# A hybrid attention block: the first attention stage in written order on four engines, the merge's gate weights loaded earlier, and a new order at the merge's head

## The chip, the cores and the metric

The kernel runs on one core of one Trainium2 chip. The metric is the device time of one execution in microseconds (us). The core's engines are PE (matmuls), DVE (vector), ACT (scalar and activation), POOL (a second, slower vector engine) and SP, which here only issues DMAs. Each engine works through its own queue in order; between queues there are semaphores.

## The reference

One layer of a decoder block over 528 positions (16 learned meta tokens ahead of 512 tokens, width 1024). One projection of the normed input feeds two attention branches of 16 heads, MLA and FoX (a forgetting attention whose logits get a cumulative gate). Each branch's output is multiplied by silu of its z, projected, gated by a sigmoid and summed:

```python
u = rmsnorm(h, pre_norm_g[l])
proj = u @ w_in[l]
(cq, ckv, k_pe_raw, z_mla, fq, fk, fv, f_logit, z_fox, gate_a, gate_b) = jnp.split(proj, split_idx, axis=-1)
...
y_mla = (o_mla * jax.nn.silu(z_mla)) @ w_br_mla[l]
...
y_fox = (o_fox * jax.nn.silu(z_fox)) @ w_br_fox[l]
mixed = (jax.nn.sigmoid(gate_a) * y_mla + jax.nn.sigmoid(gate_b) * y_fox) @ w_out[l]
h = h + rmsnorm(mixed, post_norm_g[l])
```

## The kernel before

**Numbers in two parts.** Weights and activations are split into a high and a low part, and each product is three matmul passes (high by high, high by low, low by high). A weight tile of 128 x 1024 is loaded by SP (`wload`, L133, tile `wraw`), its high part is cast by ACT (`wsplit`, L142, `wh`), and its low part is a subtraction on POOL or DVE (`split_lo`, L118, `wl`). All three tiles come from the pool `wp`, three buffers each, so that a load waits until an older tile is free.

**The stages.** After a front phase (norm, transposes, small projections) come 16 attention stages, two heads each, FoX and MLA by turns. A stage is: the scores of query blocks 0 to 2 (`scores(0)`, called s0), then of block 3 (s1): PE writes `st`, DVE takes it out with a running minimum (L665, `sf`, `nb`), ACT takes the exponentials (L673, which also sums them into `su`). Then the norm (`norm(0)`, `norm(1)`, called n0 and n1): DVE scales `su` and takes its reciprocal `ri` (L681, L682), ACT writes the high part of the weights `pn` (L700), DVE the low part (L701), POOL both parts of the meta columns (L687 to L692), and SP issues a DMA transpose `pt<-pn` for each block and head, eight in a stage (L706). The values (`values`, PE's `ov`) follow in the next stage between s0 and s1, since they need `pt`. Between these pieces PE runs the fills: steps of projections for coming stages, each step one block of matmuls. In the first stages they are z (the gates of silu: ACT and DVE make `sil` from it, L617 and L618), `mq` and `mk` (MLA queries and keys, cut into high and low, `hlq` and `hlk`, by ACT L255 and DVE L118), v, and vt (the values transposed, cut into `vp` and `vm`) and so on. A step's first matmul makes the unit's weights, and also calls the loads of the next three units.

**The rope.** `pe_unit` computes the rotated part of the queries for eight heads at a time. `rest` turns the two halves x on POOL (L544, `gT<-gT`), casts the high part on ACT (L545), splits off the low part on POOL (L118) and writes four pieces to `qpe_dram` (L548). For each pair of MLA heads `q_done` then loads `QP` from there (L507), which the scores of the next MLA stage read.

**Who sets the order.** In the attention stages PE runs in written order (`manual_schedule`), and a scheduler with priorities sets the order of the others. From the merge on, all engines run in an order written as strings of short words (`go`): w, b and u are the operands of the merge's products and of its y units (L load, S scale, q square sums, s a sum of two parts, h and l the high and low operand), G makes the next gate's weights and asks for the load of the one after, g is one step of a gate's matmuls (three of them), y a step of a y unit, M the mix of gate and y, O one of the eight units of W_out prepared ahead of the end. The gates are `pg` on PE and a tanh on ACT (L437, L449, `th`). `Weights.scale` uses `sum` (PE, ones by the partial square sums `yss`) and makes `ysc` from it on DVE (L112 and on).

Of the kernel before, what the change touches and what calls it, by code (L numbers as in the profile page):

```python
# [54 lines left out]
def block_kernel(ctx: ExitStack, tc: tile.TileContext, x, meta_tokens, pre_norm_g, w_in, fox_forget_b,  # L55
# [81 lines left out]

    def wsplit(ld, keep=None, eng=None):

        u, raw, parts, n = ld  # L140
        wh, wl = ((keep or wp).tile([128, 1024], F32R, tag=t, name=f"{t}{u}") for t in ("wh", "wl"))
        nc.scalar.copy(wh[:, :n], raw[:, :n])  # L142
        split_lo(eng or nc.gpsimd, wl[:, :n], raw[:, :n], wh[:, :n])
        return [(wh[:, o : o + w], wl[:, o : o + w]) for o, w in parts]
# [4 lines left out]
    def weights(srcs, wrap):  # L149

        st = {}

        def load():
            if "l" not in st:
                st["l"] = wload(srcs())

        def get(eng=None):
            load()
            return wrap(wsplit(st["l"], eng=eng))
        get.load = load  # L160
        return get
# [26 lines left out]
    def unit(name, getw, act, nk, sls, done):  # L188

        st = {}  # L190
        out = []
        for i, sl in enumerate(sls):
            n = sl.stop - sl.start
            for k in range(nk):
                def fn(i=i, sl=sl, k=k, n=n):
                    if "w" not in st:
                        st["w"] = getw()
                        for load in getattr(out[0][1], "nxt", ()):
                            load()
# [8 lines left out]
                out.append((3 * n / 2.4, fn))  # L208
        if hasattr(getw, "load"):
            out[0][1].load = getw.load  # L210
        return out
# [244 lines left out]


    with ExitStack() as att:

# [32 lines left out]
        wuqh = wuq.rearrange("p k (h e) -> p k h e", e=NOPE + ROPE)  # L492

        def q_mla(pr):
            kv = wukv.rearrange("p (h a e) -> p a h e", a=2, e=HD)

            def wrap(w):
                mw[pr] = w
                return (lambda k: w[k][0]), (lambda k: w[k][1])
            get = weights(lambda: [wuqh[:, k, 2 * pr : 2 * pr + 2, 0:NOPE] for k in range(2)]  # L500
                          + [kv[:, i, 2 * pr : 2 * pr + 2, :] for i in range(2)], wrap)

            halves = hl_done(("q", 0, pr), S, S)

            def q_done(i, ps):
                halves(i, ps)
                nc.sync.dma_start(f32(QP), qpe_dram[2 * pr : 2 * pr + 2].rearrange("h i x f s -> (h i x f) s"))  # L507
            return unit(f"mq{pr}", get, cq_act, 2, REAL, q_done)
# [3 lines left out]
        def pe_unit(g):  # L512
# [27 lines left out]

            def rest():

                for x in range(2):
                    nc.gpsimd.tensor_tensor(out=tt[:, x], in0=tt[:, x], in1=tt[:, 3 - x], op=(ALU.subtract, ALU.add)[x])  # L544
                    nc.scalar.copy(rr[:, x], tt[:, x])  # L545
                    split_lo(nc.gpsimd, rr[:, 2 + x], tt[:, x], rr[:, x])
                    for i in range(2):
                        nc.sync.dma_start(qpe_dram[8 * g : 8 * g + 8, i, x], f32(rr[:, 2 * i + x]))  # L548
            return out, [(0, rest)]

# [71 lines left out]
        def attention(br, pr):  # L622
# [20 lines left out]
            def scores(g):  # L643
# [4 lines left out]
                def fn():  # L648
# [4 lines left out]
                    for ib, parts in enumerate(banks):  # L653
# [5 lines left out]
                        for b, c0, w, o in parts:  # L659
                            m0 = 384 - 128 * b + c0  # L660
                            for h in range(2):
                                nb = sums["nb"][:, h, b : b + 1]

                                with tc.high_priority(offset=100):
                                    nc.vector.tensor_tensor_reduce(  # L665
                                        out=sf_of(h, b)[:, c0 : c0 + w], in0=ps[h][:, o : o + w],
                                        in1=maskt[:, m0 : m0 + w], scale=-scale, scalar=3.0e38 if c0 == 0 else nb,
                                        op0=ALU.add, op1=ALU.min, accum_out=nb)
                    with tc.high_priority(offset=60):
                        for b in GRP[g]:  # L670
                            for h in range(2):
                                sf = sf_of(h, b)
                                nc.scalar.activation(sf, sf, AF.Exp, bias=sums["nb"][:, h, b : b + 1], scale=-1.0,  # L673
                                                     accum_out=sums["su"][:, h, b : b + 1])
                return fn

            def norm(g):
                def fn():
                    b0, nb_ = GRP[g][0], len(GRP[g])
# [13 lines left out]
                    for b in GRP[g]:  # L693
                        for h in range(2):
# [3 lines left out]
                                      for i in range(2))  # L698
# [46 lines left out]
        v, vts[1, 0] = v_unit(1, 0)  # L745
        pe, pe_rest = pe_unit(0)
        first = v + gate_unit() + pe
        fills = []
        for si, (br, pr) in enumerate(stages):
# [16 lines left out]
            if si == 0:  # L766
                fill[2:2] = pe_rest
            if si == 1:
                pe, pe_rest = pe_unit(1)
                fill[9:9] = pe + pe_rest  # L770
            fills.append(fill)
# [6 lines left out]
        for si, (br, pr) in enumerate(stages):  # L778
            s0, s1, n0, n1, va = attention(br, pr)

            for fn in [s0] + late + [s1]:
                fn()

            fill = fills[si]
            run(fill[:4])
            n0()
# [14 lines left out]

    def wout_unit(n, c, keep=None):
        return by_k(wunit([wout[:, 2 * c : 2 * c + 2, 512 * n : 512 * n + 512]], keep)[0], 2)

    E_ = mybir.EngineType
    with ExitStack() as mg:
# [191 lines left out]
        def go(plan):  # L998

            for t in plan.split():  # L1000
# [28 lines left out]
                elif k == "O":  # L1029
                    pre.append(wout_unit(0, len(pre)))  # L1030
                else:
# [139 lines left out]
```

## Time and profile before

| | us |
|---|---|
| runs of the kernel before | 629.81, 633.15, 635.74 |
| median | 633.15 |
| profiled execution, its own time | 629.45 |
| its span in the trace | 627.6 |
| mean granted TensorE clock of its core | 0.996 |
| busy: PE, DVE, ACT, POOL | 601.6, 381.7, 383.4, 193.6 |

The span runs from the first to the last instruction of the trace; all times of rows are from its start. A row of the timeline has the start, the time, the engine, the line, the operation, the tiles (out<-in), the shape and the count; where the engine stood idle before it, the idle time and what ended it follow in brackets. A row with a count over 1 has the time of the whole block. The front phase ends near 56 us, the first attention stage starts near 72, the merge's head lies near 425 to 455, the y units from about 520 to 590, the last projection and norm behind them.

### The profile page before, as it was taken

The numbers are of one execution on the slowest core, as the hardware profiler recorded it, in microseconds if no ns is written. First come the engines' busy times: TensorE is split into PE (matmuls) and PEld (weight loads), VectorE is DVE, ScalarE is ACT, GpSimd is POOL, SyncE is SP. The second block draws the span as 40 slices with busy tenths as digits, with TensorE's granted clock in tenths as the row PEclk, the third lists the DMA queues.
The fourth block names the chain that finished last, engine by engine and source line by source line (L and its number), as shares of the span: only waits on it lengthen the run. The fifth ranks groups of instructions, "written<-read, shape, count | busy, mean of one in ns | idle before, by whom it ended". The sixth has DMA issues, their size and how long they took to land.

```text
span 627.6 us, 11566 instructions
## 1 busy us (share of the span) xinstructions
PE 601.6 (96%) x4058; PEld 493.9 (79%) x4058; DVE 381.7 (61%) x1013; ACT 383.4 (61%) x838; POOL 193.6 (31%) x239
## 2 busy tenths in 40 slices
PE   2999989999999999999999999999899999999996
PEld 2879767988988889889889888887688876655885
DVE  3757557377367565664774774664977774448234
ACT  5656478378477676774884785774867754245421
POOL 3334643734344353252443353410000000004700
PEclk9999989999999999999999999999999999999999
DMA  8443557866656688477467566657153128314302
GB/s 268 141 84 86 112 141 190 191 151 159 154 126 154 152 146 153 124 165 183 84 157 166 137 152 150 145 125 231 38 149 96 55 71 261 110 40 156 107 33 101
DMA packets 204865, 85.40 MB, mean 136 GB/s; under 512 B 122684, under 2 KB 197820, under 8 KB 204808
## 3 DMA queue, kind: packets, MB, share of 16 engines
q1 hardware_dynamic: 204808, 84.67, 54.2%
q8 instruction: 32, 0.52, 0.4%
q14 instruction: 25, 0.20, 0.1%
HBM read 55.21 MB, written 4.26 MB: 95 GB/s over the span
## 4 chain that ended last, share of the span: by engine, by line
PE 87%; ACT 4%; DMA 3%; DVE 2%; SPq 1%; POOL 1%; issue 1%; DVEq 0%; POOLq 0%; ACTq 0%
PE z L92 12%; PE pg L92 12%; PE v L92 8%; PE st L92 8%; PE fk L92 8%; PE po L92 7%; PE fq L92 7%; PE py L92 6%; PE ov L92 5%; PE yx L92 3%; PE psm L92 3%; PE yy L92 2%; PE mq L92 2%; PE mk L92 1%; DMA wsr<-in_w_in_dram 1%; PE vt L95 1%
## 5 line engine op out<-in xcount | busy, mean ns | idle before, releaser
L118 POOL TENSOR_TENSOR wl<-wraw,wh 128x1024 fp32r<-128x1024 f32 (+1 forms) x62 | 137.8, 2226 | 300.7 <-ACT wh L142 290.5
L142 ACT CAST wh<-wraw 128x1024 fp32r<-128x1024 f32 (+1 forms) x74 | 72.8, 987 | 82.1 <-issue 35.6
L673 ACT ACTIVATE sf<-sf,nb 128x144 f32<-128x144 f32 (+3 forms) x128 | 71.9, 565 | 3.0 <-DVE nb L665 3.0
L700 ACT ACTIVATE pn<-sf,ri 128x128 f16<-128x128 f32 (+3 forms) x128 | 61.9, 552 | 15.0 <-ACT sf L673 14.8
L701 DVE SCALAR_TENSOR_TENSOR pn<-sf,ri,pn 128x128 f16<-128x128 f32 (+3 forms) x128 | 66.0, 555 | 7.9 <-ACT pn L700 7.9
L92 PE MATMUL pg<-uTh,wh 128*128 128x512 f32 x128 | 52.1, 407 | 1.6 <-DVE ysc L112 1.6
L92 PE MATMUL z<-uTh,wh 128*128 128x512 f32 x128 | 51.4, 402 | 0.0
L92 PE MATMUL pg<-uTh,wl 128*128 128x512 f32 x128 | 50.1, 391 | 0.5 <-DVE wl L118 0.5
L92 PE MATMUL z<-uTl,wh 128*128 128x512 f32 x128 | 50.6, 395 | 0.0
L92 PE MATMUL z<-uTh,wl 128*128 128x512 f32 x128 | 50.4, 394 | 0.0
L92 PE MATMUL pg<-uTl,wh 128*128 128x512 f32 x128 | 49.9, 390 | 0.0
L665 DVE CUSTOM_DVE_ANT_0 sf<-st,maskt 128x272 f32<-128x272 f32 (+2 forms) x128 | 48.5, 435 | 0.0
L92 PE MATMUL st<-hlk,hlq 64*128 64x272 f32 (+3 forms) x480 | 47.9, 307 | 0.4 <-DVE nb L665 0.2
L92 PE MATMUL py<-g,yw 128*128 128x512 f16 x192 | 42.6, 379 | 0.6 <-DVE yw L934 0.6
L92 PEld LDWEIGHTS st<-hlk,hlq 64*128 64x128 f32 x480 | 35.3, 185 | 6.7 <-ACT wh L142 2.5
L92 PE MATMUL fk<-uTl,wh 128*128 128x256 f32 (+1 forms) x128 | 36.6, 286 | 0.0
L92 PE MATMUL fk<-uTh,wh 128*128 128x256 f32 (+1 forms) x128 | 36.5, 285 | 0.0
L92 PE MATMUL v<-uTh,wh 128*128 128x256 f32 (+1 forms) x128 | 36.5, 285 | 0.0
L92 PE MATMUL fk<-uTh,wl 128*128 128x256 f32 (+1 forms) x128 | 36.5, 285 | 0.0
L92 PE MATMUL v<-uTl,wh 128*128 128x256 f32 (+1 forms) x128 | 36.4, 285 | 0.0
L92 PE MATMUL v<-uTh,wl 128*128 128x256 f32 (+1 forms) x128 | 36.4, 284 | 0.0
L687 POOL TENSOR_TENSOR mt<-sf,ri 128x96 f32<-128x96 f32 (+1 forms) x32 | 9.5, 298 | 86.3 <-DVE ri L682 46.5
(291 smaller groups left out, 1512.0 us busy)
## 6 DMA issues: line engine op xcount, KB each, us to landing
wraw<-in_w_in_dram SPq DMA_DIRECT2D x56, 512.0 KB, 4.4
yraw<-in_w_br_fox_dram SPq DMA_DIRECT2D x8, 512.0 KB
yraw<-in_w_br_mla_dram SPq DMA_DIRECT2D x8, 512.0 KB, 4.5
wraw<-in_w_out_dram SPq DMA_DIRECT2D x8, 512.0 KB, 3.5
qpe_dram<-gT SPq DMA_DIRECT2D x8, 256.0 KB
QP<-qpe_dram SPq DMA_DIRECT2D x8, 256.0 KB, 2.8
pt<-pn SPq DMA_TRANSPOSE x128, 2.7
xr<-in_x_dram SPq DMA_DIRECT2D x4, 512.0 KB
```

What stands on the lines that cost most here:

```text
L92: nc.tensor.matmul(*a, **k)
L95: nc.tensor.transpose(*a)
L118: eng.tensor_tensor(out=lo, in0=src, in1=f32(hi), op=ALU.subtract)
L142: nc.scalar.copy(wh[:, :n], raw[:, :n])
L665: nc.vector.tensor_tensor_reduce(out=sf_of(h, b)[:, c0 : c0 + w], in0=ps[h][:, o : o + w], in1=maskt[:, m0 : m0 + w], scale=-scale, scalar ...
L673: nc.scalar.activation(sf, sf, AF.Exp, bias=sums["nb"][:, h, b : b + 1], scale=-1.0, accum_out=sums["su"][:, h, b : b + 1])
L687: nc.gpsimd.tensor_tensor(out=mt, in0=src, in1=ri.unsqueeze(3).broadcast_to([128, 2, nb_, META]), op=ALU.mult)
L700: nc.scalar.activation(hi, sf, AF.Copy, scale=rib)
L701: nc.vector.scalar_tensor_tensor(out=lo, in0=sf, scalar=rib, in1=hi, op0=ALU.mult, op1=ALU.subtract)
```

## The change

It has four parts, and the matmuls stay the same in number and shape.

1. **Stage one in written order.** For si == 0 the engines PE, POOL, ACT and DVE run in the order of the code, from the making of the weights of the first z unit to the first four fill steps. `scores` returns the exponentials as a function of their own. `pe_unit` returns `turn` (both turns of the rope on POOL, x = 1 first) and `rest(x)` (cast, low part, DMAs), which are called between the exponentials of blocks 0, 1 and 2. The weights of zb are made ahead, with the low part on DVE behind the norm of blocks 0 to 2 (`lo[0]()`). The first QP load is issued within the norm, behind the transposes of block 0.
2. **Gate weights.** Ahead of the last values, `mgates[1]` and `mgates[2]` are asked for, where it was `mgates[1]` alone.
3. **The head of the merge.** A new plan string.
4. **The y units.** The gate steps stand behind y0, y2, y4 and y5 (before: y0 to y3), G stands in y0, y2 and y4 (before: y0, y1, y2), and the O in the y units is in y5 instead of y6 with its low part on DVE instead of POOL.

```diff
-    def wsplit(ld, keep=None, eng=None):
+    def wsplit(ld, keep=None, eng=None, later=None):
...
-        split_lo(eng or nc.gpsimd, wl[:, :n], raw[:, :n], wh[:, :n])
+
+        def lo():
+            split_lo(eng or nc.gpsimd, wl[:, :n], raw[:, :n], wh[:, :n])
+        if later is None:
+            lo()
+        else:
+            later.append(lo)
...
+        def make(*a):
+            if "w" not in st:
+                st["w"] = getw(*a)
+                for load in getattr(out[0][1], "nxt", ()):
+                    load()
...
             def q_done(i, ps):
                 halves(i, ps)
-                nc.sync.dma_start(f32(QP), qpe_dram[2 * pr : 2 * pr + 2].rearrange("h i x f s -> (h i x f) s"))
+                if pr:
+                    load_qp(pr)
...
-            def rest():
-
-                for x in range(2):
+            def turn():
+
+                for x in (1, 0):
                     nc.gpsimd.tensor_tensor(out=tt[:, x], in0=tt[:, x], in1=tt[:, 3 - x], op=(ALU.subtract, ALU.add)[x])
-                    nc.scalar.copy(rr[:, x], tt[:, x])
-                    split_lo(nc.gpsimd, rr[:, 2 + x], tt[:, x], rr[:, x])
-                    for i in range(2):
-                        nc.sync.dma_start(qpe_dram[8 * g : 8 * g + 8, i, x], f32(rr[:, 2 * i + x]))
-            return out, [(0, rest)]
+
+            def rest(x):
+                nc.scalar.copy(rr[:, x], tt[:, x])
+                split_lo(nc.gpsimd, rr[:, 2 + x], tt[:, x], rr[:, x])
+                for i in range(2):
+                    nc.sync.dma_start(qpe_dram[8 * g : 8 * g + 8, i, x], f32(rr[:, 2 * i + x]))
+            return out, turn, rest
...
                     for b in GRP[g]:
+                        if b == 1:
+                            mid()
                         for h in range(2):
...
+            with ExitStack() as head:
+                if si == 0:
+                    head.enter_context(tc.manual_schedule(engines={E_.PE, E_.Pool, E_.Activation, E_.DVE}))
+                    za, q, zb = early
+                    turn, rest = rope0
+                    za.make()
+                    q.make()
+                    lo = []
+                    turn()
+                    s0()
+                    zb.make(nc.vector, lo)
+                    e0({(0, 1): lambda: rest(1), (1, 1): lambda: rest(0)})
+                    s1()
+                    n0(lambda: load_qp(0))
+                    lo[0]()
+                    e1()
+                    run(fill[:4])
...
-        mgates[1].load()
+        for g in mgates[1:3]:
+            g.load()
...
-        go("w0L w1L G b1s7 b1hA b1hB g g b1lA w0q0 g b1lB b1s6 w0q1 g g G b1s4 g g b1s5 b1hC w0S g w0s7 w0hA g w0hB b1lC g w0lA "
-           "g w0lB b1hD g w0s6 g G w0s5 w0s3 g w0hC g b1lD g w0hD g w0lC g w1q0 g w0lD g g w1q1 g g G g g g g g g g g g")
+        go("w0L b1s7 G b1hA b1hB g g b1lA w0q0 g g b1lB b1s6 g g b1s4 w0q1 G w1L g g g w0S b1hC w0s7 b1s5 g w0hA g w0hB b1lC "
+           "g w0lA g b1hD g w0lB w0s6 g G w0s5 w0s3 g w0hC b1lD g w0hD g w0lC g w1q0 g w0lD g g w1q1 g g G g g g g g g g g")
...
-            plan = (f"y{i}0 {n}L y{i}1 {j + 'S' if i else ''} y{i}2 {j}h {mix[0]} y{i}3 {j}l y{i}4 {mix[1]} y{i}5 {n}q y{i}6 {'G' if i < 3 else ''} y{i}7 "
-                    + "g " * (8 * (i < 4)) + ("O" if i == 6 else ""))
+            plan = (f"y{i}0 {n}L y{i}1 {j + 'S' if i else ''} y{i}2 {j}h {mix[0]} y{i}3 {j}l y{i}4 {mix[1]} y{i}5 {n}q y{i}6 "
+                    f"{'G' if i in (0, 2, 4) else 'O' if i == 5 else ''} y{i}7 " + "g " * (8 * (i in (0, 2, 4, 5))))
```

Three places where the rows of an engine move. (The lines of the changed file differ from those before by 11 to 45; L706 is L729 now, L548 is L566, L665 is L683, L673 is L693, L681 and L682 are L702 and L703, L701 is L722, L618 is L636, L822 is L867 and L846 is L891.)

SP, in the first attention stage, before. `wraw_1016` are weights of the second pair's keys, `CT` the cumulative gates of the FoX branch; the two transposes with 128x3x128 are block 0's, those with 5 block 1's, with 7 block 2's, with 9 block 3's:

```order
L548 DMA qpe_dram<-gT_684 8x16x512
L133 DMA wraw_1016<-in_w_in_dram 128x8x128
L548 DMA qpe_dram<-gT_684 8x16x512 x3
L269 DMA CT<-c_dram 2x528 x2
L507 DMA QP<-qpe_dram 128x512
L706 DMA_TRANSPOSE pt_661<-pn_659 128x3x128
L706 DMA_TRANSPOSE pt_662<-pn_659 128x3x128
L706 DMA_TRANSPOSE pt_661<-pn_659 128x5x128
L706 DMA_TRANSPOSE pt_662<-pn_659 128x5x128
L706 DMA_TRANSPOSE pt_661<-pn_659 128x7x128
L706 DMA_TRANSPOSE pt_662<-pn_659 128x7x128
```

The same place in the changed kernel, where `wraw_887` stands for `wraw_1016`:

```order
L566 DMA qpe_dram<-gT_684 8x16x512 x4
L280 DMA CT<-c_dram 2x528
L729 DMA_TRANSPOSE pt_661<-pn_659 128x3x128
L729 DMA_TRANSPOSE pt_662<-pn_659 128x3x128
L280 DMA CT<-c_dram 2x528
L507 DMA QP<-qpe_dram 128x512
L729 DMA_TRANSPOSE pt_661<-pn_659 128x5x128
L729 DMA_TRANSPOSE pt_662<-pn_659 128x5x128
L729 DMA_TRANSPOSE pt_661<-pn_659 128x7x128
L133 DMA wraw_887<-in_w_in_dram 128x8x128
L729 DMA_TRANSPOSE pt_662<-pn_659 128x7x128
L133 DMA wraw_1194<-in_w_in_dram 128x8x128
```

The four writes of the rope now stand together, block 0's transposes stand ahead of the QP load, and the load of `wraw_887` has moved from between the rope's writes to between block 2's two transposes; another load follows it.

DVE, from the first reciprocals of stage one to the first split of queries and keys, before:

```order
L681 TENSOR_SCALAR su_827<-su_827 128x2x3
L682 RECIPROCAL ri_828<-su_827 128x2x3
L681 TENSOR_SCALAR su_827<-su_827 128x2
L682 RECIPROCAL ri_828<-su_827 128x2
L701 SCALAR_TENSOR_TENSOR pn_659<-sf_829,ri_828,pn_659 128x128 x2
L701 SCALAR_TENSOR_TENSOR pn_659<-sf_829,ri_828,pn_659 128x2x128 x2
L701 SCALAR_TENSOR_TENSOR pn_659<-sf_829,ri_828,pn_659 128x3x128 x2
L701 SCALAR_TENSOR_TENSOR pn_660<-sf_870,ri_828,pn_660 128x4x128 x2
L618 SCALAR_TENSOR_TENSOR sil_963<-sil_963,z_903 128x512
L598 TENSOR_TENSOR vp_664<-vt_966,vp_664 128x8x64
L608 TENSOR_TENSOR vm_666<-vm_973,vm_666 16x128
L118 TENSOR_TENSOR hlq_1008<-mq_988,hlq_1008 128x512
```

The same place in the changed kernel:

```order
L703 RECIPROCAL ri_848<-su_847 128x2x3
L722 SCALAR_TENSOR_TENSOR pn_659<-sf_849,ri_848,pn_659 128x128 x2
L722 SCALAR_TENSOR_TENSOR pn_659<-sf_849,ri_848,pn_659 128x2x128 x2
L722 SCALAR_TENSOR_TENSOR pn_659<-sf_849,ri_848,pn_659 128x3x128 x2
L118 TENSOR_TENSOR wl_885<-wraw_806,wh_884 128x1024
L702 TENSOR_SCALAR su_847<-su_847 128x2
L703 RECIPROCAL ri_848<-su_847 128x2
L636 SCALAR_TENSOR_TENSOR sil_983<-sil_983,z_957 128x512
L616 TENSOR_TENSOR vp_664<-vt_986,vp_664 128x8x64
L118 TENSOR_TENSOR hlq_1005<-mq_998,hlq_1005 128x512
L626 TENSOR_TENSOR vm_666<-vm_993,vm_666 16x128
L722 SCALAR_TENSOR_TENSOR pn_660<-sf_903,ri_848,pn_660 128x4x128 x2
```

The low part of zb's weights (`wl_885`) has come in from POOL and stands behind the pn of blocks 0 to 2; the pn of block 3 (`pn_660`) has moved behind `sil`, `vp`, `hlq` and `vm`.

DVE at the head of the merge, before; `bop1` are the operands of the FoX branch, `gT` its gated values, `wl` the low part of a gate's weights:

```order
L846 SCALAR_TENSOR_TENSOR bop1A<-gT_688,gsc,bop1A 128x2048
L846 SCALAR_TENSOR_TENSOR bop1B<-gT_688,gsc,bop1B 128x1024
L822 TENSOR_TENSOR gT_688<-gT_688 128x4x256
L118 TENSOR_TENSOR wl_5630<-wraw_5601,wh_5629 128x1024
L822 TENSOR_TENSOR gT_688<-gT_688 128x4x256 x2
L112 TENSOR_SCALAR ysc_5590<-sum_5645 128x1
L114 TENSOR_SCALAR ysc_5590<-ysc_5590 128x1
L115 RECIPROCAL ysc_5590<-ysc_5590 128x1
L869 TENSOR_SCALAR ysc_5590<-ysc_5590,gsc 128x1
L822 TENSOR_TENSOR yraw_5587<-yraw_5587 128x512
L846 SCALAR_TENSOR_TENSOR bop1C<-gT_688,gsc,bop1C 128x2048
```

The same place in the changed kernel:

```order
L891 SCALAR_TENSOR_TENSOR bop1A<-gT_688,gsc,bop1A 128x2048
L891 SCALAR_TENSOR_TENSOR bop1B<-gT_688,gsc,bop1B 128x1024
L867 TENSOR_TENSOR gT_688<-gT_688 128x4x256 x2
L118 TENSOR_TENSOR wl_5632<-wraw_5517,wh_5631 128x1024
L112 TENSOR_SCALAR ysc_5595<-sum_5654 128x1
L114 TENSOR_SCALAR ysc_5595<-ysc_5595 128x1
L115 RECIPROCAL ysc_5595<-ysc_5595 128x1
L914 TENSOR_SCALAR ysc_5595<-ysc_5595,gsc 128x1
L867 TENSOR_TENSOR yraw_5592<-yraw_5592 128x512
L867 TENSOR_TENSOR gT_688<-gT_688 128x4x256
L891 SCALAR_TENSOR_TENSOR bop1C<-gT_688,gsc,bop1C 128x2048
```

Two of the `gT` sums now stand together ahead of the weights' low part, the read of `sum` (L112) follows that directly, and the third sum has moved behind the chain of `ysc`. A fourth has moved out of this place, ahead of the last attention stage's last `su`.

More of the change, by code (lines that the diff above doesn't have):

```diff
@@ L155, in load, with get @@
                 st["l"] = wload(srcs())
-        def get(eng=None):
+        def get(eng=None, later=None):
             load()
-            return wrap(wsplit(st["l"], eng=eng))
+            return wrap(wsplit(st["l"], eng=eng, later=later))
         get.load = load
@@ L195, in fn @@
                 def fn(i=i, sl=sl, k=k, n=n):
[L196 to L199, printed above, removed]
+                    make()
                     if k == 0:
@@ L208, in unit @@
                 out.append((3 * n / 2.4, fn))
+        out[0][1].make = make
         if hasattr(getw, "load"):
@@ L455, in __init__ @@
             self.steps[0][1].load = w.load
+    E_ = mybir.EngineType
     with ExitStack() as att:
@@ L492, in block_kernel, with load_qp @@
         wuqh = wuq.rearrange("p k (h e) -> p k h e", e=NOPE + ROPE)
+        def load_qp(pr):
+            nc.sync.dma_start(f32(QP), qpe_dram[2 * pr : 2 * pr + 2].rearrange("h i x f s -> (h i x f) s"))
         def q_mla(pr):
@@ L668, in fn, with ex @@
                                         op0=ALU.add, op1=ALU.min, accum_out=nb)
+                def ex(mid={}):
                     with tc.high_priority(offset=60):
@@ L674, in fn @@
                                                      accum_out=sums["su"][:, h, b : b + 1])
-                return fn
+                                mid.get((b, h), int)()
+                return fn, ex
             def norm(g):
-                def fn():
+                def fn(mid=int):
                     b0, nb_ = GRP[g][0], len(GRP[g])
@@ L745, in block_kernel @@
         v, vts[1, 0] = v_unit(1, 0)
-        pe, pe_rest = pe_unit(0)
+        pe, pe_turn, pe_rest = pe_unit(0)
         first = v + gate_unit() + pe
@@ L766, in block_kernel @@
             if si == 0:
-                fill[2:2] = pe_rest
+                early = za[0][1], q[0][1], zb[0][1]
+                rope0 = pe_turn, pe_rest
             if si == 1:
-                pe, pe_rest = pe_unit(1)
-                fill[9:9] = pe + pe_rest
+                pe, pe_turn, pe_rest = pe_unit(1)
+                fill[9:9] = pe + [(0, pe_turn)] + [(0, lambda x=x: pe_rest(x)) for x in (1, 0)]
             fills.append(fill)
@@ L778, in block_kernel @@
         for si, (br, pr) in enumerate(stages):
-            s0, s1, n0, n1, va = attention(br, pr)
-            for fn in [s0] + late + [s1]:
-                fn()
+            (s0, e0), (s1, e1), n0, n1, va = attention(br, pr)
             fill = fills[si]
-            run(fill[:4])
-            n0()
+            with ExitStack() as head:
[15 more added lines that the diff above has]
+                    run(fill[:4])
+                else:
+                    s0()
+                    e0()
+                    for fn in late:
+                        fn()
+                    s1()
+                    e1()
+                    run(fill[:4])
+                    n0()
             run(fill[4:11])
```

7 lines of the change are left out of this document (3 added, 4 removed).

## The prediction

> **What bounds the kernel now.** I read the page first, then the waits of PE, then the windows round each wait, and last the rows of each engine ahead of the wait. The page says that PE is the bound:
>
> ```profile
> PE 601.6 (96%) x4058; PEld 493.9 (79%) x4058; DVE 381.7 (61%) x1013; ACT 383.4 (61%) x838; POOL 193.6 (31%) x239
> ```
>
> The change leaves PE's matmuls as they are in number and shape, so it can only win or lose idle time of PE, or its clock. Outside the front and back phase (0 to 56 us), which the change does not touch, the list of what PE waited for has seven places of over 0.2 us (columns: us in total, times, longest):
>
> ```profile
> PE pg L92 <- DVE ysc L112: 1.6, 1, 1.6
> PE mk L92 <- DVE hlq L118: 1.6, 1, 1.6
> PE mk L92 <- DVE sil L618: 1.3, 1, 1.3
> PE ov L92 <- DMA pt<-pn: 1.1, 1, 1.1
> PE py L92 <- DVE yw L934: 0.6, 1, 0.6
> PE sum L92 <- ACT junk L100: 0.6, 1, 0.6
> PE pg L92 <- DVE wl L118: 0.5, 1, 0.5
> ```
>
> Three of them (two mk, ov) are the first attention stage, three (sum, two pg) the head of the merge, one (py) the y units. That is 7.3 us together, and a clock loss comes on top. The windows show it (columns: us, then the busy time of PE, PEld, DVE, ACT, POOL, then PE's clock, DMA share, GB/s):
>
> ```profile
> 90.00:95.00 5.00, 4.99 (x20) 4.30 (x21) 1.79 (x6) 0.99 (x2) 1.38 (x2) 0.68 0.55 123
> ```
>
> Behind the two mk waits PE is busy, but at a granted clock of 0.68; at half clock that is 3.2 of the 5 us ((1 - 0.68) / 0.5 x 5). PE's own rows give the loss from start to start:
>
> ```profile
> 86.08 0.39 PE L92 MATMUL z<-uTh,wl 128*128 128x512 f32 x1
> 87.80 0.39 PE L92 MATMUL mk<-cTh,wh 128*128 128x272 f32 x1 [1.33 <-DVE sil L618]
> 88.15 0.29 PE L92 MATMUL mk<-cTh,wl 128*128 128x272 f32 x1
> 90.01 0.58 PE L92 MATMUL mk<-cTh,wh 128*128 128x256 f32 x1 [1.57 <-DVE hlq L118]
> 91.24 0.63 PE L92 MATMUL z<-uTl,wh 128*128 128x512 f32 x1
> 91.67 0.63 PE L92 MATMUL z<-uTh,wl 128*128 128x512 f32 x1
> 94.25 0.39 PE L92 MATMUL z<-uTl,wh 128*128 128x512 f32 x1
> 94.48 0.40 PE L92 MATMUL z<-uTh,wl 128*128 128x512 f32 x1
> 97.83 0.38 PE L92 MATMUL ov<-pt,vm 80*64 80x512 f16 x1
> 99.31 2.00 PE L92 MATMUL ov<-pt,vp 128*64 128x512 f16 x24
> ```
>
> A z matmul follows the last after 0.23 us at full clock (94.25, 94.48) and after 0.43 at the low one (91.24, 91.67). So 87.80 is 1.49 late (86.08 + 0.23 = 86.31), 90.01 is 1.73 late (88.15 + 0.13 = 88.28), the low clock costs 0.20 on each of some seven z and a little on the mk, together 1.6, and the values (ov), due some 0.1 behind 97.83, are 1.3 late. In all 6.1 us in one stage.
>
> **Why the first stage stalls.** Two chains, on two queues:
>
> ```profile
> 73.90 2.38 POOL L118 TENSOR_TENSOR wl<-wraw,wh 128x1024 fp32r<-128x1024 f32 x1
> 77.49 2.55 POOL L118 TENSOR_TENSOR gT<-gT,gT 128x512 fp32r<-128x512 f32 x2
> 73.32 0.08 DVE L665 DVE_READ_ACCUMULATOR2_ANT nb<- 128x1 f32 x1
> 77.58 0.62 ACT L545 CAST gT<-gT 128x512 fp32r<-128x512 f32 x1 [2.98 <-POOL gT L544]
> 78.10 0.41 ACT L673 ACTIVATE sf<-sf,nb 128x144 f32<-128x144 f32 x1
> 81.28 0.17 DVE L681 TENSOR_SCALAR su<-su 128x6 f32<-128x6 f32 x1 [4.32 <-ACT sf L673]
> 83.01 4.13 DVE L701 SCALAR_TENSOR_TENSOR pn<-sf,ri,pn 128x128 f16<-128x128 f32 x8
> 87.06 0.68 DVE L618 SCALAR_TENSOR_TENSOR sil<-sil,z 128x512 f32<-128x512 f32 x1
> ```
>
> POOL splits zb's weights (2.38) between the two turns of the rope (gT). ACT stands 2.98 us for the second turn with the exps queued behind its cast, though the first of them could start at 73.4 (nb); six exps, 78.10 to 81.28, take 3.2. DVE then stands 4.32 for the exps, does eight pn in one block of 4.13, and only then sil (87.06) and hlq, for which PE waits. The other chain is SP's:
>
> ```profile
> 76.31 0.37 SPq L133 DMA_DIRECT2D wraw<-in_w_in_dram  x1
> 78.22 3.04 SPq L548 DMA_DIRECT2D qpe_dram<-gT  x3
> 85.93 0.35 SPq L507 DMA_DIRECT2D QP<-qpe_dram  x1
> 86.39 11.20 SPq L706 DMA_TRANSPOSE pt<-pn  x8
> SPq L507 <- DMA qpe_dram<-gT: 3.7, 1, 3.7
> wraw<-in_w_in_dram SPq DMA_DIRECT2D x56, 512.0 KB, 4.4
> ```
>
> The last rope write needs the second split (77.49 + 2.55 = 80.0); the QP load stands for its landing until 85.9; behind it are all eight transposes, at 1.40 each until 97.6, and ov starts 1.72 later.
>
> **The change, stage one.** POOL's wl goes to DVE, so the second split ends about 2.38 earlier, taken as 77.7; the last rope write lands at 83.5 (same 5.9 from split to landing). The first two transposes now stand ahead of the QP load. They need only two pn pairs: with the exps no longer behind the second cast (3.2 for six exps and 0.5 for each of two casts between them, from 73.5) su comes at 77.8, 3.5 earlier, and the pair goes out by 79.8, done by 82.6, so QP is again bound by the landing, 83.5. Behind it stand six transposes (8.40) and, new, two weight loads (0.4 each to issue): 83.9 + 8.4 + 0.8 = 93.1, against 97.6 before. ov starts at 99.31 - 4.5 = 94.8. PE would reach it, without the mk waits and the low clock (4.8), at about 93.1, so 1.6 us of wait stay at ov: the gain is 4.5, not 6.1.
>
> Do the mk waits go? DVE: su 77.8, six of eight pn at about 0.5 each, wl 1.2 (82.5), su and ri of block 3, sil at 83.6 to 84.3, hlq by 86. PE needs sil at 86.3 and hlq at 88.3. The last pn pair (some 1.4) now stands behind hlq; its cover is SP, which needs it only for its last two transposes at about 90. zb's wl is wanted by the third matmul of zb's second part, at 84.0; it has 1.5 us of cover.
>
> A rule speaks against this wl. The Trainium skill (GPSIMD Engine Reference, Specifications) says that GpSimd and VectorE share SBUF interfaces, and that VectorE instructions with two SBUF inputs contend. This trace agrees elsewhere:
>
> ```profile
> 572.64 5.16 POOL L118 TENSOR_TENSOR wl<-wraw,wh 128x1024 fp32r<-128x1024 f32 x2 [156.41 <-ACT wh L142]
> 573.71 1.88 DVE L948 SCALAR_TENSOR_TENSOR th<-th,ysc,th 128x512 f32<-128x512 f32 x1
> 526.93 0.74 DVE L948 SCALAR_TENSOR_TENSOR th<-th,ysc,th 128x512 f32<-128x512 f32 x1
> ```
>
> The same th takes 1.88 beside POOL's wl and 0.74 alone. If the moved wl fell beside POOL work and took 2.5 times as long (1.2 to 3.1), it would end at 84.4 and cost PE 0.4. By my order POOL's meta parts are done by then; the sum takes 0.
>
> What it gives back: the load of the second key weights, issued at 76.3 before, now stands behind three more transposes, at about 88. With its landing (4.4 by the last row above) and a cast of 1.05, ACT reaches the next sil at about 93.5, and the exps of stage two start near 95 where a full shift would put them at 93.4. PE has stage two's fills as cover; I take 0.5 (0 to 1.8, the whole delay). Stage one: -4.0. Bounds: -6.1 if ov no longer waits, -2.3 if only the 2.3 of the earlier rope write come through.
>
> **The change, head of the merge.** The rows ahead of the 1.6 wait:
>
> ```profile
> 431.06 9.21 SPq L133 DMA_DIRECT2D wraw<-in_w_in_dram  x4
> 437.57 1.05 ACT L142 CAST wh<-wraw 128x1024 fp32r<-128x1024 f32 x1 [3.27 <-DMA wraw<-in_w_in_dram]
> 438.66 1.23 DVE L118 TENSOR_TENSOR wl<-wraw,wh 128x1024 fp32r<-128x1024 f32 x1 [4.86 <-ACT wh L142]
> ```
>
> The weights were asked for at 431.06 and ACT stood 3.27 for them, DVE 4.86 for ACT, and the read that frees PE's accumulator (ysc, L112) came behind all that on DVE. Now this load is issued ahead of the last stage's transposes, over 20 us early: both stands go, L112 comes up to 4.86 earlier against 1.8 needed (the 1.6 wait, from start to start). The sum's matmuls move six matmuls later (1.4 us), more than the 0.6 wait. The 0.5 for the next wl goes if it keeps the shift; that one is close. From start to start the three are 0.7 + 1.8 + 0.7 = 3.2. I take -3.0 (-1.5 if two of the small ones come back, -3.2 at most). The extra load ahead of the last transposes costs SP 0.4 in a stretch where it stood waiting for pn: nothing. One gT sum (L822) goes ahead of the last stage's last su on DVE, where DVE waits for exps: nothing.
>
> **The y units and the end.** Which gate group stands where changes; the py wait came from this:
>
> ```profile
> 559.78 0.60 ACT L449 ACTIVATE th<-pg 128x512 f32<-128x512 f32 x1 [7.39 <-DVE th L948]
> ```
>
> ACT holds a tanh ahead of the next yw. It bites where no gate group (24 matmuls of 0.23, 5.5 us) follows the unit. The change takes the groups from behind y1 and y3 and puts them behind y4 and y5: the wait goes at y4 and comes up at y1 to y2, with the same rows. 0 (-0.6 to +0.6). The first W_out unit splits on DVE instead of POOL: 0 (to +1, the end's PE being fed by POOL's splits).
>
> **Sum.** -4.0 - 3.0 + 0 = -7.0 against the profiled execution: 629.45 (span 627.6) to 622.4. The median of the runs shown, 633.15, stands 3.7 above it, and the runs spread 629.81 to 635.74; the same gain taken off the median is 626.2 us, -1.1%. What a measurement here can tell from no change is about 1%, so the forecast lies on the border.
>
> **Rivals.** (1) *The transposes hardly move.* If the QP load waits longer, because the rope writes now share the rings with the other loads, or the two weight loads delay the landings behind them, and the late exps cost the full 1.8: stage one gives 4.5 - 0.8 - 1.8 = 1.9, merge 2.5, total -4.4: 628.8. For it: this queue is what ov waits for in both orders. Against: the landing moves with the split. (2) *All of the idle time goes*: -6.1 and -3.2: 633.15 - 9.3 = 623.8. It needs the transposes 1.6 faster than my sum. (3) *Slower: the written order holds everything behind one late landing.* The place is SP's QP load with six transposes and the next weights behind it. Total zero is reached if the rope write lands 7.0 later than 83.5, at 90.5; then ov, the weights' cast, sil and the exps of stage two slide one for one, and the low clock (1.6) returns. At 10 later the time is 633.15 + 3.0 + 1.6 = 637.8. The row has 5.9 from split to landing, so this needs nearly three times that. (4) *The low clock returns while all else is right.* The ov wait of 1.6 is shorter than the two mk waits (2.9) which preceded the clock's drop, so by the rows it stays at 1.00; if not, +1.6: 627.8. The Trainium skill (TensorE: Matmul & The Clock Gate, What's actually happening) puts the drop after an idle window of about 3.4 us that runs free of the kernel; the low stretch here (3.2) is nearly of that length, and by that rule 1.6 us of idle would not suffice.
>
> **How the numbers follow.** Forecast 0.60, rival 1 0.17, rival 2 0.10, rival 3 0.05, rival 4 0.08. With a scatter of about 2.5 us of a median, the forecast lies below 626.8 (1% faster) in 0.6 of its cases, rival 2 nearly always, rivals 1 and 4 in a fifth to a third: 0.36 + 0.09 + 0.06 = 0.51 faster. Rival 3 beyond +1% (639.5) is 0.03. The rest, 0.46, is within 1%. The range runs from rival 2 less its scatter, 621.5, to rival 1 with its scatter, 631.3.
>
> **What would show it.** Right: in the profile after, no mk wait and clock 1.00 from 85 to 95; transposes beginning near 80 in two groups with QP between them, ending near 93; ov near 95 with a wait of 1 to 2; L112 without a stand of DVE at the merge's head; a py wait of 0.6 near the second y unit. Wrong: an mk wait for sil or hlq, st waits for nb in stage two of over 1 us, a new wait for wl at the merge's head, or po waits at the end.

## The result and the profile after

The changed kernel takes 627.89 us (median of 11 runs, 626.45 to 628.64) against 630.72 for the kernel before (11 runs, 629.32 to 635.74). The ratio of the means is 0.9938, with a 95% interval of 0.9915 to 0.9960: it is faster, by 0.4% to 0.85%. That is a gain of 3.9 us (2.5 to 5.4), where 7.0 was forecast; the medians differ by 2.8 and the profiled executions by 2.5 (spans 627.6 and 625.1). The gain is under 1%: the prediction had given this a chance of 0.46, and 0.51 to more than 1%. The time lies in the range that was given, but the range (621.5 to 631.3) holds the median of the kernel before as well, and the base of the forecast, a median of three runs (633.15), was 2.4 us above the median of eleven.

The list of what PE waited for in the changed kernel (without the front phase; line numbers of the changed file):

```profile
PE ov L92 <- DMA pt<-pn: 5.2, 2, 4.8
PE py L92 <- DVE yw L979: 0.6, 1, 0.6
PE st L92 <- DVE nb L683: 0.3, 1, 0.3
```

Both mk waits are gone, and all three waits at the merge's head. One wait has grown: the values of stage one (ov) wait 5.2 us for their transposes, where it was 1.1. The windows show what that cost (columns as before: time, busy time of PE, PEld, DVE, ACT, POOL, PE's clock, DMA share, GB/s):

```profile
85.00:90.00 5.00, 5.00 (x30) 4.08 (x28) 3.90 (x12) 1.91 (x4) 1.17 (x2) 1.00 0.68 165
90.00:95.00 5.00, 2.33 (x31) 2.00 (x30) 0.00 (x0) 1.30 (x2) 0.91 (x3) 1.00 0.99 230
95.00:100.00 5.00, 2.46 (x11) 1.20 (x13) 3.21 (x15) 4.25 (x16) 2.24 (x2) 0.61 1.19 288
100.00:105.00 5.00, 5.00 (x43) 4.29 (x40) 2.91 (x11) 2.38 (x6) 1.10 (x4) 0.71 0.17 38
```

From 85 to 90 PE is full and at full clock, as forecast. Then it is idle for over half of 90 to 100, while the DMA engines are full, and from 95 to 105 its clock is 0.61 and 0.71. So the hole and the slow clock behind it have moved 5 to 10 us later and have not become smaller. PE's rows and SP's, in the same stage:

```profile
75.37 0.50 PE L92 MATMUL z<-uTh,wh 128*128 128x512 f32 x1
97.12 0.60 PE L92 MATMUL ov<-pt,vm 80*64 80x512 f16 x1 [4.79 <-DMA pt<-pn]
98.15 3.80 PE L92 MATMUL ov<-pt,vp 128*64 128x512 f16 x24
103.74 0.51 PE L92 MATMUL fq<-uTh,wh 128*128 128x512 f32 x1
419.56 0.25 PE L92 MATMUL sum<-gss,ALL 128*128 128x1 bf16 x4
```

```profile
78.94 4.14 SPq L729 DMA_TRANSPOSE pt<-pn  x2
84.84 0.36 SPq L507 DMA_DIRECT2D QP<-qpe_dram  x1
85.27 3.88 SPq L729 DMA_TRANSPOSE pt<-pn  x3
89.26 0.52 SPq L133 DMA_DIRECT2D wraw<-in_w_in_dram  x1
89.87 1.25 SPq L729 DMA_TRANSPOSE pt<-pn  x1
91.22 0.53 SPq L133 DMA_DIRECT2D wraw<-in_w_in_dram  x1
91.83 4.12 SPq L729 DMA_TRANSPOSE pt<-pn  x2
```

The 24 matmuls of ov take 3.80 at the low clock (2.00 before). SP's last two transposes, right behind the second weight load, take 2.06 each; the three at 85.27 took 1.29 each.

For all runs the program can be cut at three rows of PE: the first z matmul of stage one, the first ov<-pt,vp of stage one, and the sum of `gss` near the merge's head (419.56 above). The table has the time from z to ov, from z to that sum (nearly all of the stages), and from the sum to the end of the span. What lies ahead of the first z is left out: z starts between 75.4 and 77.2 in these executions, and the starts differ by 1.2 among those whose code up to there is the same. Each row comes from one execution; each ratio is to runs of the kernel before taken beside it (medians 630.7 to 632.1).

| kernel | ratio to before (95%) | z to ov | z to the sum | the sum to the end |
|---|---|---|---|---|
| before | | 23.3 | 342.2 | 209.3 |
| the change | 0.9938 (0.9915 to 0.9960) | 22.8 | 344.2 | 205.5 |
| e1_merge | 0.9948 (0.9926 to 0.9971) | 23.9 | 342.7 | 205.6 |
| e2_stage | 1.0005 (0.9985 to 1.0024) | 22.7 | 343.5 | 210.6 |
| e9_gates | 0.9946 (0.9925 to 0.9967) | 23.2 | 342.2 | 205.7 |
| e10_head | 0.9947 (0.9922 to 0.9973) | 24.0 | 342.8 | 205.6 |
| e11_y | 0.9994 (0.9977 to 1.0011) | 24.0 | 344.3 | 209.0 |
| e4_one | 0.9917 (0.9890 to 0.9944) | 21.1 | 341.4 | 205.6 |
| e3_behind | 0.9927 (0.9901 to 0.9953) | 19.0 | 342.0 | 205.7 |
| e5_qp | 0.9907 (0.9877 to 0.9938) | 18.8 | 342.5 | 205.6 |
| e8_exps | 0.9876 (0.9849 to 0.9904) | 20.6 | 341.2 | 205.6 |
| e7_early | 0.9871 (0.9844 to 0.9898) | 19.5 | 338.6 | 206.4 |

In the profiled executions the merge and what follows gained 3.8, the stages lost 2.0, and what lies ahead of z was 0.7 shorter, which is within its scatter: together the 2.5. The 3.8 is clear: with the old merge the last column is 209.0 to 210.6, with the new one 205.5 to 206.4. The 2.0 is not: in the five executions whose stage one is that of the kernel before (before, e1, e9, e10, e11) z to the sum takes 342.2 to 344.3.

### The profile page after: what moved, and what is told of

The parts are those of the page before. It is cut to its first block, busy times and chain, and to the rows that moved or that the text cites. A ratio compares the mean times of both kernels' runs of the same rounds, so it can differ in the third digit from the quotient of the medians.

```text
span 625.1 us, 11556 instructions
## 1 busy us (share of the span) xinstructions
PE 601.1 (96%) x4058; PEld 494.2 (79%) x4058; DVE 380.8 (61%) x1015; ACT 384.7 (62%) x838; POOL 188.9 (30%) x237
## 4 chain that ended last, share of the span: by engine, by line
PE 92%; DVE 2%; ACT 2%; DMA 2%; SPq 1%; issue 0%; DVEq 0%; ACTq 0%
PE pg L92 14%; PE z L92 14%; PE v L92 8%; PE st L92 8%; PE fk L92 8%; PE po L92 7%; PE fq L92 7%; PE py L92 6%; PE ov L92 5%; PE yx L92 3%; PE psm L92 3%; PE mq L92 2%; PE yy L92 2%; PE vt L95 1%; PE mk L92 1%; DMA wsr<-in_w_in_dram 1%
## 5 line engine op out<-in xcount | busy, mean ns | idle before, releaser
L118 POOL TENSOR_TENSOR wl<-wraw,wh 128x1024 fp32r<-128x1024 f32 (+1 forms) x60 | 132.9, 2219 | 298.7 <-ACT wh L142 284.3
L693 ACT ACTIVATE sf<-sf,nb 128x144 f32<-128x144 f32 (+3 forms) x128 | 71.9, 565 | 6.1 <-DVE nb L683 6.1
L722 DVE SCALAR_TENSOR_TENSOR pn<-sf,ri,pn 128x128 f16<-128x128 f32 (+3 forms) x128 | 65.7, 553 | 7.6 <-ACT pn L721 7.6
L683 DVE CUSTOM_DVE_ANT_0 sf<-st,maskt 128x272 f32<-128x272 f32 (+2 forms) x128 | 48.5, 435 | 0.1
```

Of the source, the lines that this page charges most:

```text
L118: eng.tensor_tensor(out=lo, in0=src, in1=f32(hi), op=ALU.subtract)
L683: nc.vector.tensor_tensor_reduce(out=sf_of(h, b)[:, c0 : c0 + w], in0=ps[h][:, o : o + w], in1=maskt[:, m0 : m0 + w], scale=-scale, scalar ...
L722: nc.vector.scalar_tensor_tensor(out=lo, in0=sf, scalar=rib, in1=hi, op0=ALU.mult, op1=ALU.subtract)
```

## The experiments

The theory after the result (A): the change gains about 3 us at the merge's head and loses 1 to 2 in stage one, because two weight loads of 0.5 MB have come to stand among the transposes that ov waits for. The rivals were that stage one is where the gain comes from (B), that the QP load's wait for the rope is what makes the transposes late (C), and that ACT and DVE are late for the weights (D).

**e1_merge and e2_stage, one half each.** e1 is the kernel before with parts 2 to 4, e2 the kernel before with part 1.

> The kernel before with parts 2 to 4 of the change alone (the gate loads, the merge's head, the y units); stage one as before. Theory A (the merge's head gives what was forecast, stage one gives some of it back): 3.0 us faster than before, ratio near 0.995, so no slower than the whole change. Rival B (the gain of the whole change comes from stage one, the merge's waits being replaced by others): within 1 us of before.

> The kernel before with part 1 alone, stage one in written order. Theory A: stage one loses, since the values start later against PE's own work and the low clock that follows the longer wait falls on them: 0.5 to 2 us slower than before. Rival B: 2 to 4 us faster than before.

e1 measured 0.9948, e2 1.0005. The gain is the merge's, and stage one in written order brings nothing that can be told: the 95% interval of e2 is within 0.25% of no change (0.9 us faster to 1.5 slower). Rival B is out. That stage one makes the kernel slower, as theory A expected of e2, is not shown: the 1.3 us that e2's execution and the 2.0 that the whole change's took longer from z to the sum lie within the scatter of that span. What is the same in both is the place: ov comes 22.7 and 22.8 behind z, where 18.7 was forecast.

**e9_gates, e10_head and e11_y, the merge's three parts apart.**

```diff
 e9:
-        mgates[1].load()
+        for g in mgates[1:3]:
+            g.load()
 e10: the plan string of the merge's head alone
 e11: the plan of the y units and the W_out unit on DVE alone
```

> The kernel before with part 2 alone: two gates' weights asked for ahead of the last values. Theory A (the late weights held ACT and DVE, and through them the read that frees PE's accumulator): the wait of pg for ysc (1.6) goes, the small waits (sum, wl) may stay, 1.5 to 2.5 us faster than before. Rival G (the new plan string does the work): less than 0.7 us.

> The kernel before with part 3 alone: the new plan string at the merge's head, with the second gate's weights asked for as before. Theory A: the sum wait goes (0.7), the read of the sum still stands behind the late weights on DVE, so the ysc wait stays: 0.5 to 1.2 us faster than before. Rival G: 2 to 3 us faster.

> The kernel before with part 4 alone: the gate groups behind y0, y2, y4 and y5, and the W_out unit one earlier with its low part on DVE. Theory A (the py wait only moves): one py wait of 0.6 near the second y unit in place of the one near the fifth, no new wait at the end, within 0.7 us of before. Rival H: 0.6 to 1 us faster, or a po wait and up to 1 us slower.

e9 measured 0.9946, e10 0.9947, e11 0.9994. The expectation for e10 missed, and the one for e9 was too low (about 3.4 us instead of 1.5 to 2.5): the plan string alone gives as much as the early loads alone, and as both together (e1). Neither is added to the other. The rows of e10 show how (SP, ACT and DVE):

```profile
429.23 3.24 SPq L133 DMA_DIRECT2D wraw<-in_w_in_dram  x2
436.24 1.05 ACT L142 CAST wh<-wraw 128x1024 fp32r<-128x1024 f32 x1 [0.28 <-DMA wraw<-in_w_in_dram]
437.32 1.23 DVE L118 TENSOR_TENSOR wl<-wraw,wh 128x1024 fp32r<-128x1024 f32 x1 [0.99 <-ACT wh L142]
438.46 0.15 DVE L112 TENSOR_SCALAR ysc<-sum 128x1 int32<-128x1 int32 x1
```

In the new plan the second pair of yraw loads (`w1L`) stands behind the gate's load, so that the gate's load goes two transfers earlier; both sums of `gT` come before the weights; and L112 follows the weights' low part directly. ACT stands 0.28 for the weights, where it was 3.27. Which of these the wait needed was not tried apart. In e9 the order is the old one and the weights are simply there: ACT casts at 434.64, right behind its last square sum:

```profile
434.64 1.03 ACT L142 CAST wh<-wraw 128x1024 fp32r<-128x1024 f32 x1
439.12 0.15 DVE L112 TENSOR_SCALAR ysc<-sum 128x1 int32<-128x1 int32 x1
```

In both, none of the three waits at the merge's head is left. In e11 the py wait of 0.6 moved, as expected, and nothing came up at the end.

**e3_behind, both weight loads behind the transposes.** The load of the second pair's keys is kept from zb's `make` and called behind `n1`, and both loads get an order edge to the last transpose (`tc.issue_after`):

```diff
+                    fk, zb.nxt = zb.nxt[2], zb.nxt[:2]
                     zb.make(nc.vector, lo)
...
             n1()
+            if si == 0:
+                behind = last_t[0].ins
+                with tc.issue_after(behind):
+                    fk()
...
+                    if si == 1:
+                        with tc.issue_after(behind):
+                            run(fill[:4])
```

> The whole change, with the two weight loads that stood among stage one's last transposes put behind all eight. Theory A (the loads, 0.5 MB each, hold up the transposes that stand behind them): the last transposes are issued by 93.5 instead of 96 and land in about 2 to 3 us, ov's second half starts near 95 instead of 98.2, and the time falls by 3 to 5 us against the whole change, to about 623 to 625. Rival C (the transposes are late because the QP load ahead of six of them waits for the rope's landing): ov moves by less than 1 us and the time stays within 1 us of the whole change's. Rival D (ACT and DVE of stage two are what is late, because the weights land later still): the time rises by 1 to 2 us.

The place was as theory A said: six transposes in a row, ov 3.8 us earlier against z than in the change (19.0 instead of 22.8), and no low clock there:

```profile
85.57 8.03 SPq L729 DMA_TRANSPOSE pt<-pn  x6
95.35 2.00 PE L92 MATMUL ov<-pt,vp 128*64 128x512 f16 x24
97.42 1.05 ACT L142 CAST wh<-wraw 128x1024 fp32r<-128x1024 f32 x1 [5.09 <-DMA wraw<-in_w_in_dram]
101.55 0.17 DVE L702 TENSOR_SCALAR su<-su 128x6 f32<-128x6 f32 x1 [6.69 <-ACT sf L693]
103.59 0.66 PE L95 MATMUL vt<-ident,vT 128*128 128x128 f32 x4 [2.54 <-DVE nb L683]
104.69 0.63 PE L92 MATMUL fq<-uTl,wh 128*128 128x512 f32 x1
```

But the time was 0.9927 (626.63 us), which can't be told from the change's 0.9938, where 3 to 5 us less were expected: the delay that rival D named was there as well. The cast of the late weights stands on ACT ahead of stage two's exps, ACT stands 5.09 for the load, DVE 6.69 for the exps, and PE 2.54 for DVE; and behind that the clock is low again (fq matmuls of 0.63).

**e5_qp, the QP load behind block 1 as well.** `mid()` is called at block 2 instead of block 1, with an order edge to the transposes before it.

> As the run with the loads behind, and the QP load moved behind block 1's transposes as well, so that only four transposes stand behind it. If the loads alone held the transposes (theory A), this gives nothing more than that run, within 0.7 us. If the wait of the QP load for the rope counts too (theory C), ov's second half starts another 1.5 to 2 us earlier, near 93.5, and the time falls by another 1 to 2 us.

ov came at 18.8 against z, 0.2 earlier than in e3 and not 1.5 to 2, and the time was 0.9907, with an interval that overlaps e3's: rival C is out, the QP load's place is worth nothing that can be told.

**e4_one, only the second load behind the transposes.** The second load is held back as in e3. The first is called behind the split on DVE and ahead of the QP load, without an order edge; on SP it is issued where it was, between block 2's two transposes.

> The whole change, with only the second of the two weight loads (the one ahead of block 3's transposes) put behind all transposes; the first stays between block 2's two. Theory A (each load holds the transposes queued behind it): ov's second half comes 1 to 2 us earlier, near 96.5, and the low clock may stay; the time falls by 1 to 2 us against the whole change, between that and the run with both loads behind. Rival I (the first load alone holds them): ov stays within 0.5 of 98.2 and the time within 0.7 us of the whole change's.

ov came at 21.1 against z, between the change's 22.8 and e3's 19.0: 1.7 us less without the second load, 2.1 less again without the first. In time the three (0.9938, 0.9917, 0.9927) can't be told apart. The three transposes behind the first load:

```profile
90.59 0.52 SPq L133 DMA_DIRECT2D wraw<-in_w_in_dram  x1
91.20 4.83 SPq L729 DMA_TRANSPOSE pt<-pn  x3
```

1.61 each, where e3 has 1.34. Not all of the differences at ov belong to the loads: QP, which stands ahead of them in the queue, was issued 9.5 behind z in the change, 9.3 in e4 and 8.8 in e3. From QP's issue to ov it takes 13.3, 11.8 and 10.2. So each load delays ov by about 1.5 us, not by the 0.4 that its issue takes. The Trainium skill (DMA: Bandwidth & Descriptors, Queues, rings and completion order) says that the DMAs of one engine's queue run on one ring per DMA engine, taken in ring order; these rows agree with it, if a transpose waits until the load's packets ahead of it on the same rings have gone; that wait itself has no row.

**e8_exps, the late cast behind the exps.** As e5, and the step that makes the second pair's key weights, with their cast on ACT, gets an order edge to stage two's sixth exp.

> As the run with the QP load behind block 1 (both weight loads behind all transposes), with the cast of the second pair's key weights put behind stage two's six exps in ACT's order. Theory A (that cast, which stands 5 us for its load with the exps queued behind it, makes the vt wait and the low clock after it): the exps run from 93.5 to 97, the vt wait goes, the clock stays at 1.00, and the time is 3 to 4.5 us below the run with the QP load behind block 1, near 621.5. Rival F (the weights themselves are late, wherever their cast stands): fk or vt waits 2 us or more for them and the time stays within 1 us of that run's.

```profile
92.53 0.41 ACT L693 ACTIVATE sf<-sf,nb 128x144 f32<-128x144 f32 x1 [0.62 <-DVE nb L683]
96.55 3.68 PE L92 MATMUL ov<-pt,vp 128*64 128x512 f16 x24
98.35 1.04 ACT L142 CAST wh<-wraw 128x1024 fp32r<-128x1024 f32 x1 [2.69 <-DMA wraw<-in_w_in_dram]
```

It measured 0.9876 (624.5 us), 0.3% below e5 with intervals that overlap. The vt wait is gone and the exps run from 92.53, as theory A had it, while the cast waits behind them. The low clock and a longer ov wait came all the same in the profiled execution (ov at 96.55, 1.8 later against z than in e5, with the same place of the transposes in SP's order), so the expected 3 to 4.5 us did not come. The windows show where the 1.8 went (columns as before, the last is GB/s):

```profile
92.50:93.00 0.50, 0.43 (x6) 0.10 (x2) 0.50 (x3) 0.47 (x3) 0.00 (x0) 1.00 0.00 0
93.00:93.50 0.50, 0.00 (x0) 0.00 (x0) 0.50 (x5) 0.50 (x4) 0.00 (x0) 1.00 0.04 3
93.50:94.00 0.50, 0.00 (x0) 0.00 (x0) 0.50 (x3) 0.50 (x4) 0.00 (x0) 1.00 0.09 10
```

For 1.5 us the DMA engines moved next to nothing, while the last transposes were being issued (four took 6.64, in e5 5.37) and before any load was. What stopped them is open. So a delay of this size can come in one execution without a load; the two loads' delay stands on two executions with the same code (22.8 and 22.7), the single load's on one.

**e7_early, the first load ahead of six transposes.** As e5, with the first load right behind block 0's two transposes, when the split on DVE has freed its buffer, and the six others behind it.

> As the run with the QP load behind block 1, with the load of the second pair's key weights put right behind block 0's transposes (issue near 84, when the split on DVE has freed its buffer) instead of behind all transposes; the other load stays behind them. Theory A (a load holds up the transposes queued behind it, and the late cast of these weights on ACT holds up stage two's exps): the cast comes near 90 instead of 97.4, the exps of stage two run from 93 to 97, the new wait of vt for nb (2.8) goes, and the six transposes behind the load lose 0 to 2 us at their front but are through by 94, so ov's second half starts at 95 to 96: 3 to 4 us faster than the run with the QP load behind block 1, near 622. Rival E (a load anywhere ahead of the transposes costs ov its whole 4.4 us): ov's second half at 97 to 99, the time at 625 to 628, like the whole change.

```profile
83.90 0.41 SPq L135 DMA_DIRECT2D wraw<-in_w_in_dram  x1
84.85 2.54 SPq L734 DMA_TRANSPOSE pt<-pn  x2
87.44 0.57 SPq L509 DMA_DIRECT2D QP<-qpe_dram  x1
88.10 5.36 SPq L734 DMA_TRANSPOSE pt<-pn  x4
90.15 1.05 ACT L144 CAST wh<-wraw 128x1024 fp32r<-128x1024 f32 x1 [0.65 <-PE z L92]
92.67 0.41 ACT L695 ACTIVATE sf<-sf,nb 128x144 f32<-128x144 f32 x1 [0.24 <-DVE nb L685]
95.18 2.00 PE L92 MATMUL ov<-pt,vp 128*64 128x512 f16 x24
98.52 0.50 PE L92 MATMUL fq<-uTh,wh 128*128 128x512 f32 x1
```

The same load, 5.4 us earlier in SP's queue, cost ov 0.7 in this execution (19.5 against 18.8 in e5): the transposes behind it go at 1.27 and 1.34 each, ov comes 3.2 us earlier than in the change against z, the cast is done by 91.2 and waits for PE and not for a load, the exps start at 92.67 instead of 96.22, and the clock stays at 1.00 in all windows from 85 to 110. From z to the sum it takes 338.6, which is 3.6 less than before. The time is 623.58 us, 0.9871 (0.9844 to 0.9898), faster than both kernels: its interval lies below the whole change's. Rival E is out; the 3 to 4 us against e5 are not clear, as the two intervals overlap.

## Why the prediction was right and wrong

**What bounds, and the mk waits: right.** PE was the bound, and only its holes and its clock moved. The mk waits went, with sil at 82.87 and hlq at 84.36 on DVE where 83.6 to 84.3 and 86 were forecast, and the low clock behind them.

**The moved split: right.** DVE's wl took 1.21 us at 80.56 with POOL's meta parts done at 78.9; the contention that the rule would have given did not come up there.

**The transposes: wrong, and this is the step that failed.** The working put "two weight loads (0.4 each to issue)" among six transposes and reached ov at 94.8, 18.7 behind z's 76.06. It came at 22.8, 4.0 late. Half of this lies behind QP's issue: 13.3 to ov in the change, where 11.3 was forecast, and 10.2 in e3 without the loads. So the term of 0.8 was about 3.1, some 1.5 for each load. That is near what 512 KB take at the 230 to 290 GB/s that the windows from 90 to 100 show (an estimate: 1.8 to 2.3 us), and far from the issue; the 4.4 from issue to landing, which the prediction had used for the cast, would have been too much. The other half lies ahead: QP was to be issued 7.4 behind z, 5.9 after the split on POOL, and came at 9.5 in the change and 8.8 in e3. The split was in time:

```profile
74.47 2.60 POOL L118 TENSOR_TENSOR gT<-gT,gT 128x512 fp32r<-128x512 f32 x2
```

From its end at 77.07 to QP at 84.84 are 7.8. The first two transposes, which SP issues meanwhile, took 2.07 each, where 1.4 had been reckoned. Moving QP back (e5) brought ov only 0.2 earlier, so QP's own stand is not what cost this half; why landing and first transposes took longer stays open.

**The low clock: wrong.** Removing the mk waits was credited with 1.6 of clock, and rival 4 held a wait of 1.6 at ov for too short to bring it back. The wait became 4.8 + 0.4, and the low clock came back over ov and the scores: 3.80 for ov's 24 matmuls instead of 2.00. Against a forecast of -4.0 the stages up to the merge measured +2.0 in the profiled execution and e2, stage one alone, +0.3 (-0.9 to +1.5) in time.

**The give-back: the mechanism right, its cover wrong.** The exps of stage two did start late for the weights' cast (96.22). In the change this was hidden behind the longer ov wait; as soon as that is taken away (e3) it costs 2.5 us and a low clock. With the load early (e7) it is gone, and stage one gives -3.6 in that one execution, near the -4.0 of the sum, by an order of loads that the change doesn't have.

**The merge's head: right in size, half right in cause.** Forecast -3.0, measured -3.7 from the sum to the end in e1, and 0.9948 in time (-3.3 us, -1.8 to -4.7). The working put it down to the early load; the plan string alone does it as well.

**The y units: right.** The wait moved (528.33 in the changed kernel, 0.59 long), e11 is 0.9994.

**The rivals.** Rival 1 came nearest, and named both causes (the QP load waits longer, or "the two weight loads delay the landings behind them"), but its price (0.8 and the exps' 1.8) was too small: it left stage one 1.9 of gain where none can be told. That its total of 628.8 and the forecast's 626.2 lie on either side of the 627.89 is luck: both were taken off a base 2.4 us too high, and the merge gave 3.3 where rival 1 had 2.5.

## What to carry to other kernels

When a change moves DMAs in a queue, a load can cost what stands behind it far more than its issue: about 1.5 us each here, not 0.4. Price it by its bytes at the rate that the windows show, and look which transfer behind it has a reader that waits; 5 us earlier in the queue (e7) the same load cost its reader 0.7. A written order on the engines leaves the DMA queue's order to whoever sets it; here the gain of stage one came only when the loads had been moved. Two edits that remove the same wait are not added up: try each alone.

## What the runs showed of the hardware

The clock fell after shorter idle stretches than the prediction had counted on. In e11, whose stage one is that of the kernel before, the usual low stretch at 90 to 95 was followed by a second one:

```profile
95.00:100.00 5.00, 3.27 (x36) 2.33 (x36) 3.22 (x16) 4.36 (x13) 3.62 (x3) 1.00 0.80 172
100.00:105.00 5.00, 5.00 (x46) 3.90 (x46) 1.91 (x6) 3.57 (x10) 1.15 (x4) 0.66 0.94 258
```

PE was idle for 1.7 of the 5 us ahead of it, in waits of 0.65 and 1.08. e1 has the same rows there with waits of 0.55 and 1.09 and a clock of 1.00. So the same idle time brings the low clock in one execution and not in another, and it cost e11 some 1.5 us (ov's 24 matmuls took 3.47). The Trainium skill (TensorE: Matmul & The Clock Gate, What's actually happening) speaks of an idle window of about 3.4 us that runs free of the kernel; a free run would fit what is seen, the length of the idle time does not: these waits are shorter, and matmuls lie between them.
